# The second token block's seven Strassen factors: split ahead of time into scratch instead of at the block boundary

## The chip, the cores and the metric

One core of a Trainium2 chip runs the whole kernel. The metric is the device time of one execution in microseconds (us). Five engines work side by side and meet through semaphores: TensorE (PE, with its weight loads PEld) multiplies, VectorE (DVE) and GpSimd (POOL) do elementwise work, ScalarE (ACT) does copies and functions, SyncE (SP) issues the transfers between HBM and the on-chip memory (SBUF). Every engine takes its own instructions strictly in the order in which they were laid down.

## The reference, cut to what matters

A decoder layer: LayerNorm, a mixer (sliding-window attention beside gated linear attention), LayerNorm, then a SwiGLU feed-forward and a last LayerNorm. The change lies in the feed-forward's first half:

```python
def swiglu(h, w_gate, w_up, w_down):
    a = jax.nn.silu(jnp.einsum('bld,df->blf', h, w_gate)) * jnp.einsum('bld,df->blf', h, w_up)
    return jnp.einsum('blf,fd->bld', a, w_down)
```

Here h has 2048 tokens of 1024 features, and the gate and up matrices have 2816 columns each. All of it is float32.

## The kernel before, in words

**Two parts of a number.** A float32 value x is written as the sum of two: hi, a copy of x rounded by ACT into the type float32r, and lo = x - hi, made by DVE or POOL. A product of two such values takes three matmuls (hi hi, hi lo, lo hi). `split_into` (L182) makes both parts: its line 183 is the ACT copy, line 184 the subtraction. Nearly all splits of the kernel are counted under these two lines, so the profile's rows are told apart by the names of their tiles.

**Blocks and pairs.** The gate and up products run over two token blocks (`tb` 0 and 1) of 1024 tokens. Within a block the loop at L1411 runs over 11 *pairs* (`p`), each a group of 256 columns of the gate and of the up matrix. A pair is a Strassen-Winograd scheme: the block's activations, cut into four quarters (two halves of the features by two halves of the tokens, 512 tokens each), give seven *factors*: three quarters as they are (b11, b21, b22) and four sums or differences (t1 to t4). The weights give seven others (a11, ps2, ps1, a12, ps3, a22, ps4). `product(f)` (L1420) multiplies one factor of the activations by one of the weights: 24 matmuls of 128x128 by 128x512. The order of a pair is b11, t2, t1, b21, t3, t4, b22. DVE adds the results out of PSUM (`add`, L1435), `gate` (L1384) makes four gated activations out of them, POOL makes three further sums and one difference (L1477 to L1483), and all of it is stored for the second half of the feed-forward.

**Where the factors live.** A factor of the activations holds both its parts for four feature tiles: [128, 2, 4, 512], 2 MB. All seven lie in SBUF for a whole block. The quarters come from `n_scT`, the normalised activations, transposed, in HBM. Sums for the second block are made early by `combine_later` (L660): in the pairs p = 2 to 5 of the first block, one feature tile per pair, four quarters of [128, 512] are loaded into `cb` buffers (four of them, pool `hop4`), DVE makes the four sums in place (L671), and they are stored unsplit to `t_sc`.

**The block boundary.** In the last pair of the first block, right after `product(f)` has used a factor for the last time, `make(f, 1)` (L678) fills its place anew: for each of the four feature tiles a raw [128, 512] row is loaded into a `cb` buffer (L701 for b11, b21, b22 from `n_scT`; L704 for t1 to t4 from `t_sc`), ACT copies hi into the factor's place, and lo is made there by POOL for tiles 0 and 2 and by DVE for tiles 1 and 3 (L707). That is 28 loads, 28 copies, 14 subtractions on POOL and 14 on DVE for the seven factors.

**The weights.** `fetch_weights` (L1349) loads the four raw quarters of the next pair (512 KB each), `weights` (L1357) makes the seven factors of them: POOL does four sums (L1369, L1373) and the lo of four factors, DVE the lo of three (ps1, ps3, ps4; L1377, L1379, L1382), ACT all seven hi. Four buffers (`whl`) hold them, so they are made only a few products ahead. The profile calls the factors split from raw quarters `pa` and the others `ps`.

**What sets the order.** The framework's scheduler reorders instructions across the program by a timing model and then fixes one order per engine; instructions passed to `tc.keep_in_program_order` keep their order among themselves. All transfers of this stage go through SP's single queue, where an entry that waits (for a buffer or for its data) holds up those behind it. Results of `gate` and of the sums lie in three staging buffers (`sa`, `sb`, `sc`), so `sa` of a pair can be written only once the stores from the last pair's `sa` have landed.

Of the kernel before, what the change touches and what calls it, by code (L numbers as in the profile page):

```python
# [14 lines left out]
P = 128  # L15
# [108 lines left out]
def body(ctx, tc, t, seq):  # L124
# [11 lines left out]
    HT = TF // 2  # L136
    NTB = seq // TF
    NT = HT // P
    t_sc = [dr.tile([2, P, KT // 2, 2, HT], F32, name=f"t_sc{n}") for n in range(NTB)]

    a_sc = [[dr.tile([P, NTB, HT], F32, name=f"a_sc{i}_{p}") for p in range(NP)] for i in range(6)]
    a_last = [dr.tile([P, NP, HT], F32, name=f"a_last{n}") for n in range(NTB)]
# [494 lines left out]
    def combine(tb, k, tile_):  # L637

        def load(kh, th):
            x = tile_(f"cb{tb}_{k}_{kh}{th}")  # L640
            nc.sync.dma_start(x, quarter(tb, kh, th, k, 1)[:, 0, :])
            return x

        if tb > 0:
            yield from combine_later(tb, k, tile_)
            return
# [12 lines left out]

    def combine_later(tb, k, tile_):  # L660

        x = {}
        for kh, th in ((1, 1), (0, 1), (0, 0), (1, 0)):
            y = x[kh, th] = tile_(f"cb{tb}_{k}_{kh}{th}")
            tc.keep_in_program_order(nc.sync.dma_start(y, quarter(tb, kh, th, k, 1)[:, 0, :]))
        yield
        b22, b12, b11, b21 = x.values()
        for f, o, a, b, how in (("t3", b22, b22, b12, ALU.subtract), ("t1", b12, b12, b11, ALU.subtract),
                                ("t2", b11, b11, b22, ALU.add), ("t4", b21, b21, b11, ALU.subtract)):
            i, j = COMBINED[f]  # L670
            tc.keep_in_program_order(nc.vector.tensor_tensor(o, a, b, op=how))  # L671
            nc.sync.dma_start(t_sc[tb][i, :, k, j], o)
        yield
# [4 lines left out]
    def make(f, tb):  # L678

        if f in FIRST:  # L680
            x = hb.tile([P, 2, KT // 2, HT], F32R, tag="h16", name=f"h_{f}_{tb}", bufs=2)
        else:
            pool = pools["hop1" if f in EARLY else "hop3" if f == "b22" else "hop2"]
            x = pool.tile([P, 2, KT // 2, HT], F32R, tag=f"h_{f}", name=f"h_{f}_{tb}", bufs=1)
        if f in FIRST and tb == 0:
            for k in range(0, KT // 2, 2):
                raw = staging(f"r_{f}{tb}_{k}").rearrange("p (k q) -> p k q", q=HT)
                if f in SOURCE:
                    nc.sync.dma_start(raw, quarter(tb, *SOURCE[f], k, 2))
                else:  # L690
                    i, j = COMBINED[f]
                    nc.sync.dma_start(raw, t_sc[tb][i, :, k : k + 2, j])
                split_into(x[:, 0, k : k + 2], x[:, 1, k : k + 2], raw, nc.vector)
            return x
        for k in range(KT // 2):
            if tb > 0:
                raw = pools["hop4"].tile([P, HT], F32, tag="cb", name=f"r_{f}{tb}_{k}", bufs=4)
            else:
                raw = pools["hop1"].tile([P, HT], F32, tag="mk", name=f"r_{f}{tb}_{k}", bufs=3)
            if f in SOURCE:  # L700
                row_ = nc.sync.dma_start(raw, quarter(tb, *SOURCE[f], k, 1)[:, 0, :])  # L701
            else:
                i, j = COMBINED[f]
                row_ = nc.sync.dma_start(raw, t_sc[tb][i, :, k, j])  # L704
            if tb > 0:
                tc.keep_in_program_order(row_)
            split_into(x[:, 0, k], x[:, 1, k], raw, nc.vector if k % 2 else nc.gpsimd)  # L707
        return x

# [379 lines left out]
    for s in range(NSB):  # L1089
# [4 lines left out]
        for what in (MIXING_STEPS if nxt else LAST_STEPS).split():  # L1094
# [7 lines left out]
                start_ffn(int(what[1]))  # L1102
            elif what[0] == "C":
                if s == NSB - 2:
                    for _ in combine(0, int(what[1]), lambda n: op_.tile([P, HT], F32, tag="nt", name=n, bufs=3)):
                        pass
            else:
                take(what, nxt)
        pj = nxt
# [235 lines left out]
    hops2 = ctx.enter_context(ExitStack())  # L1345
    c2 = ctx.enter_context(ExitStack())
    quarters = {}

    def fetch_weights(p, tb):  # L1349

# [60 lines left out]
    for tb in range(NTB):  # L1411
        for p in range(NP):
# [24 lines left out]
                    nc.vector.tensor_tensor(o[i], x[i], y[i], op=ALU.add)  # L1437

            p1, u2, u4 = tl("p1", "p1"), tl("u2", "u2"), tl("u4", "u4")
            combined_ = None  # L1440
            if tb == 0 and NTB > 1 and 2 <= p < 2 + KT // 2:
                combined_ = combine(1, p - 2, lambda n: pools["hop4"].tile([P, HT], F32, tag="cb", name=n, bufs=4))
                next(combined_)
            for o, x in zip(p1, product("b11")):
                nc.scalar.activation(o, x, AF.Copy)
            add(u2, p1, product("t2"))
            add(u4, u2, product("t1"))
            add(p1, p1, product("b21"))
            if p + 1 < NP:
                fetch_weights(p + 1, tb)  # L1450
            elif tb + 1 < NTB:
# [74 lines left out]
```

## Time and profile before

| what | value |
|---|---|
| median of three runs | 2270.1 us (2267.31 to 2276.69) |
| the profiled execution's own time | 2267.38 us |
| its span in the trace | 2265.6 us |
| granted TensorE clock, mean | 0.986 |
| PE / DVE / ACT / POOL busy, whole span | 96% / 66% / 37% / 56% |

Times below are us from the start of the span unless it says otherwise. The feed-forward's first block runs up to about 1405, its second block from there to 1833.5, and the down projection follows. In a row of stretches the busy time of an engine is followed by its number of instructions; in rows of groups stand the instruction count, the busy time and the mean of one in ns, then the idle time before them and what ended it.

### The profile page before, as it was taken

The numbers are of one execution on the slowest core, as the hardware profiler recorded it, in microseconds if no ns is written. First come the engines' busy times: TensorE is split into PE (matmuls) and PEld (weight loads), VectorE is DVE, ScalarE is ACT, GpSimd is POOL, SyncE is SP. The second block draws the span as 40 slices with busy tenths as digits, with TensorE's granted clock in tenths as the row PEclk, the third lists the DMA queues.
The fourth block names the chain that finished last, engine by engine and source line by source line (L and its number), as shares of the span: only waits on it lengthen the run. The fifth ranks groups of instructions, "written<-read, shape, count | busy, mean of one in ns | idle before, by whom it ended". The sixth has DMA issues, their size and how long they took to land.

```text
span 2265.6 us, 31576 instructions
## 1 busy us (share of the span) xinstructions
PE 2170.6 (96%) x11536; PEld 1863.0 (82%) x11536; DVE 1501.0 (66%) x2437; ACT 833.8 (37%) x1450; POOL 1260.5 (56%) x974
## 2 busy tenths in 40 slices
PE   6899999999999999899999999999999999999998
PEld 5787888888899989777888888788888888888886
DVE  6665554566755678457899667876656555775687
ACT  4444554444243342343232323332222232222343
POOL 5765554564615243238877667877675634553433
PEclk9999999999999999999999999999999999999999
DMA  9868584564778586862535234333232278656463
GB/s 322 312 228 283 187 285 142 179 253 156 282 245 303 186 305 245 297 222 72 186 130 172 93 116 163 124 132 110 100 107 100 96 264 297 228 216 229 162 235 124
DMA packets 179628, 446.75 MB, mean 197 GB/s; under 512 B 16609, under 2 KB 62594, under 8 KB 167186
## 3 DMA queue, kind: packets, MB, share of 16 engines
q1 hardware_dynamic: 175666, 442.30, 56.0%
q10 hardware_dynamic: 3808, 2.45, 0.3%
q8 instruction: 91, 1.49, 0.3%
q14 instruction: 63, 0.52, 0.1%
HBM read 299.85 MB, written 144.83 MB: 196 GB/s over the span
## 4 chain that ended last, share of the span: by engine, by line
PE 45%; DVE 4%; POOL 2%; issue 2%; DMA 1%; ACT 0%; SPq 0%; POOLq 0%; DVEq 0%; ACTq 0%
PE t L195 17%; PE d L1234 16%; PE b L195 13%; DVE A L184 1%; DVE y L1140 1%; DMA r_b<-n_scT 1%; DMA r_t<-t_sc 1%; POOL pa L184 0%; DVE h_t L184 0%; DVE y L1315 0%; DVE B L184 0%; POOL a L1369 0%; POOL s L1373 0%; DVE y L1286 0%; DVE y L1309 0%
## 5 line engine op out<-in xcount | busy, mean ns | idle before, releaser
L1234 PE MATMUL d<-B,A 128*128 128x512 f32 x1848 | 419.7, 389 | 1.3 <-DVE y L1140 1.1
L1234 PEld LDWEIGHTS d<-B,A 128*128 128x128 f32 x1848 | 346.7, 188 | 74.1 <-DVE y L1140 1.6
L195 PE MATMUL t<-h_t,ps 128*128 128x512 f32 x1584 | 369.6, 391 | 2.3 <-ACT ps L183 1.8
L195 PEld LDWEIGHTS t<-h_t,ps 128*128 128x128 f32 x1584 | 298.0, 189 | 65.7 <-ACT ps L183 2.8
L195 PE MATMUL pu<-h,hl_u 128*128 128x512 f32 (+1 forms) x1008 | 245.7, 389 | 4.7 <-ACT h L183 3.5
L195 PE MATMUL b<-h_b,pa 128*128 128x512 f32 x1032 | 244.9, 393 | 4.3 <-POOL pa L184 4.3
L195 PEld LDWEIGHTS b<-h_b,pa 128*128 128x128 f32 x1032 | 195.3, 190 | 46.0 <-POOL pa L184 5.2
L184 POOL TENSOR_TENSOR pa<-a,pa 128x1024 fp32r<-128x1024 f32 x65 | 169.5, 2610 | 113.5 <-ACT pa L183 113.5
L195 PEld LDWEIGHTS pu<-h,hl_u 128*128 128x128 f32 x1008 | 178.5, 191 | 35.9 <-ACT h L183 4.1
L195 PE MATMUL po<-hl_o,msh 128*128 128x256 f32 x1024 | 199.9, 289 | 5.6 <-DVE yo L801 4.0
L184 DVE TENSOR_TENSOR A<-rA,A 128x1024 fp32r<-128x1024 f32 (+1 forms) x78 | 117.5, 1531 | 103.9 <-ACT A L183 103.9
L195 PEld LDWEIGHTS po<-hl_o,msh 128*128 128x128 f32 x1024 | 162.6, 191 | 7.3 <-DVE yo L801 6.0
L183 ACT ACTIVATE A<-rA 128x1024 fp32r<-128x1024 f32 (+1 forms) x78 | 78.7, 1042 | 212.5 <-PE d L1234 188.3
L195 PE MATMUL po<-hl_o,msl 128*128 128x256 f32 x512 | 147.3, 288 | 0.0
L1437 DVE TENSOR_TENSOR u<-u,t 128x512 f32<-128x512 f32 x132 | 89.3, 679 | 66.2 <-PE t L195 66.0
L195 PE MATMUL b<-h_b,ps 128*128 128x512 f32 x528 | 125.4, 393 | 4.9 <-ACT h_b L183 4.8
L195 PE MATMUL t<-h_t,pa 128*128 128x512 f32 x528 | 124.1, 390 | 1.2 <-POOL pa L184 1.2
L1369 POOL TENSOR_TENSOR a<-a,a 128x1024 f32<-128x1024 f32 x44 | 124.3, 2825 | 1.6
L195 PEld LDWEIGHTS b<-h_b,ps 128*128 128x128 f32 x528 | 99.8, 190 | 26.6 <-ACT h_b L183 5.0
L195 PEld LDWEIGHTS t<-h_t,pa 128*128 128x128 f32 x528 | 98.9, 188 | 22.5 <-POOL pa L184 2.0
L184 DVE TENSOR_TENSOR ps<-a,ps 128x1024 fp32r<-128x1024 f32 x44 | 82.0, 1863 | 46.2 <-ACT ps L183 46.2
L183 ACT ACTIVATE ps<-a 128x1024 fp32r<-128x1024 f32 x66 | 69.8, 1058 | 105.4 <-PE t L195 70.4
(321 smaller groups left out, 4365.6 us busy)
## 6 DMA issues: line engine op xcount, KB each, us to landing
a<-w_gu SPq DMA_DIRECT2D x88, 512.0 KB, 4.4
hl_u<-w_u SPq DMA_DIRECT2D x42, 1024.0 KB, 6.2
rA<-a_sc SPq DMA_DIRECT2D x66, 512.0 KB, 4.9
w<-w_d SPq DMA_DIRECT2D x50, 512.0 KB, 4.8
hl_o<-w_o SPq DMA_DIRECT2D x24, 1024.0 KB, 7.8
hT_sc<-h SPq DMA_DIRECT2D x32, 512.0 KB, 6.6
gh<-hT_sc SPq DMA_DIRECT2D x16, 1024.0 KB, 10.4
w_u<-hl_u SPq DMA_DIRECT2D x14, 1024.0 KB, 8.3
```

The costliest lines, as they stand in the source:

```text
L183: nc.scalar.activation(hi, src, AF.Copy)
L184: (lo_eng or nc.vector).tensor_tensor(lo, src, r32(hi), op=ALU.subtract)
L195: nc.tensor.matmul(out, l, r, start=(i == 0), stop=(i == n - 1))
L1140: return (eng or nc.vector).tensor_tensor(o, x, y, op=ALU.add)
L1234: nc.tensor.matmul(pt, a_[:, a, ca], fb[:, b, cb], start=(p == 0 and j == 0), stop=(p == NP - 1 and j == 2))
L1369: sub = lambda o, x, y: nc.gpsimd.tensor_tensor(o, x, y, op=ALU.subtract)
L1437: nc.vector.tensor_tensor(o[i], x[i], y[i], op=ALU.add)
```

## The change

The two parts of all seven factors of the second block are made during the first block and kept in HBM scratch; the boundary only loads them.

- A generator `factors_later` takes one feature tile (row k, four in all) per two pairs, over the pairs p = 1 to 8; the function `later` advances it three times in a pair: before b11, after b21 and after b22.
- In the odd pair it loads three quarters (b11, b21, b22), splits them (hi by ACT into one of the three `mk` buffers of pool `hop1`, lo by DVE in place in the `cb` buffer) and stores hi and lo to a scratch tensor `f_sc` per factor; then it loads four quarters for the sums. In the even pair it makes the four sums (DVE), then splits t1 and t4 and stores them; after b21 it splits t3 and t2 and stores them.
- `make(f, 1)` issues two loads of 1 MB straight into the factor's place, with no copy and no subtraction.
- `combine_later` and the second block's `t_sc` go. `combine` for the first block is a plain function now and does what it did.

```diff
-    t_sc = [dr.tile([2, P, KT // 2, 2, HT], F32, name=f"t_sc{n}") for n in range(NTB)]
+    t_sc = [dr.tile([2, P, KT // 2, 2, HT], F32, name="t_sc0")]
+    f_sc = {f: dr.tile([P, 2, KT // 2, HT], F32, name=f"f_sc_{f}") for f in ("b11", "b21", "b22", "t1", "t2", "t3", "t4")}
...
-    def combine_later(tb, k, tile_):
...
+    def factors_later(tb):
+        held = tc.keep_in_program_order
+
+        def load(k, which):
+            x = {}
+            for kh, th in which:
+                y = x[kh, th] = pools["hop4"].tile([P, HT], F32, tag="cb", name=f"cb{tb}_{k}_{kh}{th}_{len(which)}", bufs=4)
+                held(nc.sync.dma_start(y, quarter(tb, kh, th, k, 1)[:, 0, :]))
+            return x
+
+        def part(f, k, x):
+            y = pools["hop1"].tile([P, HT], F32R, tag="mk", name=f"hi_{f}{tb}_{k}", bufs=3)
+            lo = x.bitcast(F32R)
+            held(nc.scalar.activation(y, x, AF.Copy))
+            held(nc.vector.tensor_tensor(lo, x, r32(y), op=ALU.subtract))
+            for a, z in enumerate((r32(y), x)):
+                nc.sync.dma_start(f_sc[f][:, a, k, :], z)
+
+        def sums(x, which):
+            b22, b12, b11, b21 = x.values()
+            for f, o, a, b, how in (("t3", b22, b22, b12, ALU.subtract), ("t1", b12, b12, b11, ALU.subtract),
+                                    ("t2", b11, b11, b22, ALU.add), ("t4", b21, b21, b11, ALU.subtract)):
+                if f in which:
+                    held(nc.vector.tensor_tensor(o, a, b, op=how))
+                    yield f, o
+
+        for k in range(KT // 2):
+            x = load(k, ((0, 0), (1, 0), (1, 1)))
+            yield
+            for f, at_ in SOURCE.items():
+                part(f, k, x[at_])
+            yield
+            x = load(k, ((1, 1), (0, 1), (0, 0), (1, 0)))
+            yield
+            made = dict(sums(x, ("t3", "t1", "t2", "t4")))
+            for f in ("t1", "t4"):
+                part(f, k, made[f])
+            yield
+            for f in ("t3", "t2"):
+                part(f, k, made[f])
+            yield
+            yield
...
+        if tb > 0:
+            for k in range(0, KT // 2, 2):
+                tc.keep_in_program_order(nc.sync.dma_start(r32(x)[:, :, k : k + 2, :], f_sc[f][:, :, k : k + 2, :]))
+            return x
         for k in range(KT // 2):
-            if tb > 0:
-                raw = pools["hop4"].tile([P, HT], F32, tag="cb", name=f"r_{f}{tb}_{k}", bufs=4)
-            else:
-                raw = pools["hop1"].tile([P, HT], F32, tag="mk", name=f"r_{f}{tb}_{k}", bufs=3)
+            raw = pools["hop1"].tile([P, HT], F32, tag="mk", name=f"r_{f}{tb}_{k}", bufs=3)
...
             p1, u2, u4 = tl("p1", "p1"), tl("u2", "u2"), tl("u4", "u4")
-            combined_ = None
-            if tb == 0 and NTB > 1 and 2 <= p < 2 + KT // 2:
-                combined_ = combine(1, p - 2, lambda n: pools["hop4"].tile([P, HT], F32, tag="cb", name=n, bufs=4))
-                next(combined_)
+            def later():
+                if tb == 0 and NTB > 1 and p > 0:
+                    next(later_, None)
+
+            later()
             for o, x in zip(p1, product("b11")):
                 nc.scalar.activation(o, x, AF.Copy)
             add(u2, p1, product("t2"))
             add(u4, u2, product("t1"))
             add(p1, p1, product("b21"))
+            later()
...
             add(u4, u4, product("b22"))
-            if combined_ is not None:
-                next(combined_)
+            later()
```

More of the change, by code (lines that the diff above doesn't have):

```diff
@@ L642, in load @@
             return x
-        if tb > 0:
-            yield from combine_later(tb, k, tile_)
-            return
         def op(f, o, x, y, how):
@@ L658, in combine @@
         op("t4", b21, b21, b11, ALU.subtract)
-    def combine_later(tb, k, tile_):
[L662 to L673, printed above, removed]
+    def factors_later(tb):
[36 more added lines that the diff above has]
+            yield
@@ L1104, in body @@
                 if s == NSB - 2:
-                    for _ in combine(0, int(what[1]), lambda n: op_.tile([P, HT], F32, tag="nt", name=n, bufs=3)):
-                        pass
+                    combine(0, int(what[1]), lambda n: op_.tile([P, HT], F32, tag="nt", name=n, bufs=3))
             else:
@@ L1347, in body @@
     quarters = {}
+    later_ = factors_later(1)
     def fetch_weights(p, tb):
```

7 lines of the change are left out of this document (2 added, 5 removed).

## The prediction, made before the change was run

> **What bounds the kernel now.** I read the page's head first, then busy time by stretches, then the PE's own order of time at the block boundary, then who was waited for.
>
> ```profile
> span 2265.6 us, 31576 instructions
> PE 2170.6 (96%) x11536; PEld 1863.0 (82%) x11536; DVE 1501.0 (66%) x2437; ACT 833.8 (37%) x1450; POOL 1260.5 (56%) x974
> ```
>
> The PE is the bound, so an edit elsewhere pays only where the PE stands still. The stretches below are one pair long or nearly so: the fourth pair with early sums, one without, the last pair of the first block, and two longer stretches that hold the first two pairs of the second.
>
> ```profile
> 1176.80:1214.80 38.00, 38.00 (x169) 31.50 (x168) 34.49 (x30) 10.94 (x13) 27.39 (x13) 1.00 0.47 160
> 1291.00:1329.00 38.00, 38.00 (x169) 31.48 (x168) 23.94 (x26) 10.94 (x13) 25.82 (x13) 1.00 0.30 105
> 1367.00:1405.04 38.04, 38.04 (x170) 31.50 (x169) 24.49 (x24) 15.42 (x22) 32.37 (x18) 1.00 0.53 174
> 1405.04:1449.00 43.96, 40.17 (x164) 32.37 (x163) 37.51 (x29) 18.37 (x27) 37.91 (x20) 0.92 0.53 173
> 1449.00:1491.00 42.00, 40.28 (x177) 32.68 (x176) 33.51 (x33) 12.72 (x17) 32.59 (x14) 1.00 0.31 111
> ```
>
> Columns: length, then busy time of PE, PEld, DVE, ACT, POOL, the granted clock, the DMA share, GB/s. In the first block's pairs the PE is busy all the time, with the sums (DVE 34.49 of 38) or without (23.94). It idles only in the last two rows. There the PE's order of time gives the loss product by product; a healthy product lasts 1372.39 - 1366.95 = 5.44 us.
>
> ```profile
> 1366.95 5.60 PE L195 MATMUL b<-h_b,pa 128*128 128x512 f32 x24
> 1372.39 11.04 PE L195 MATMUL t<-h_t,ps 128*128 128x512 f32 x48
> ...
> 1421.36 0.61 PE L195 MATMUL b<-h_b,pa 128*128 128x512 f32 x2
> 1425.14 7.99 PE L195 MATMUL b<-h_b,pa 128*128 128x512 f32 x22 [3.17 <-POOL pa L184]
> 1432.97 5.60 PE L195 MATMUL t<-h_t,ps 128*128 128x512 f32 x24
> 1438.41 0.61 PE L195 MATMUL t<-h_t,pa 128*128 128x512 f32 x2
> 1439.64 5.28 PE L195 MATMUL t<-h_t,pa 128*128 128x512 f32 x22 [0.62 <-POOL pa L184]
> 1444.76 5.60 PE L195 MATMUL b<-h_b,ps 128*128 128x512 f32 x24
> ...
> 1466.52 0.61 PE L195 MATMUL b<-h_b,pa 128*128 128x512 f32 x2
> 1468.31 5.28 PE L195 MATMUL b<-h_b,pa 128*128 128x512 f32 x22 [1.18 <-POOL pa L184]
> 1473.43 5.60 PE L195 MATMUL t<-h_t,ps 128*128 128x512 f32 x24
> 1478.87 0.61 PE L195 MATMUL t<-h_t,pa 128*128 128x512 f32 x2
> 1480.03 5.32 PE L195 MATMUL t<-h_t,pa 128*128 128x512 f32 x22 [0.54 <-POOL pa L184]
> 1485.19 5.60 PE L195 MATMUL b<-h_b,ps 128*128 128x512 f32 x24
> ```
>
> Four products are late, all for a weight's lo (`pa`) from POOL. The first takes 1432.97 - 1421.36 = 11.61 us, 6.17 too many: 3.17 waiting, most of the rest because the 22 matmuls after the wait take 7.99 us where 24 usually end in 5.60 (the granted clock of that stretch is 0.92). The second takes 6.35 (0.91 too many), the third 6.91 (1.47), the fourth 6.32 (0.88). Together 9.4 us. That is the whole prize: 0.41% of the median.
>
> What made POOL late is seen in its groups, and DVE's, from 1376 to 1445:
>
> ```profile
> L184 POOL TENSOR_TENSOR h_t<-r_t,h_t 128x512 fp32r<-128x512 f32 x8 | 13.9, 1754 | 2.5 <-ACT h_t L183 2.5
> L184 POOL TENSOR_TENSOR h_b<-r_b,h_b 128x512 fp32r<-128x512 f32 x6 | 9.9, 1649 | 7.9 <-ACT h_b L183 7.9
> L184 DVE TENSOR_TENSOR h_t<-r_t,h_t 128x512 fp32r<-128x512 f32 x8 | 14.0, 1760 | 3.2 <-ACT h_t L183 3.2
> L184 DVE TENSOR_TENSOR h_b<-r_b,h_b 128x512 fp32r<-128x512 f32 x6 | 8.9, 1477 | 3.2 <-ACT h_b L183 3.2
> ```
>
> The 14 lo of the second block's factors on POOL cost 13.9 + 9.9 = 23.8 us there, and the POOL idles only 12 us in a plain pair (38.00 - 25.82). The same on DVE costs 22.9 us.
>
> **The change part by part.** *Removed at the boundary:* those 28 subtractions and 28 copies. Without 23.8 us of foreign work POOL is back at its plain 25.82 of 38 and its `pa` in time. Term 1: -9.4 us, bounds -9.4 (nothing else is lost there) and -7.1 (the third and fourth delays stay, below).
>
> *Added at the boundary:* 14 loads of 1 MB, each released by the end of a product. Seven factors of 2.1 MB are 14.7 MB; with one pair's weights (4 x 512 KB) and seven stores (256 KB) it is 18.6 MB, asked for within one pair.
>
> ```profile
> 704.00:708.00 4.00, 4.00 (x36) 4.00 (x35) 1.67 (x7) 1.36 (x2) 0.00 (x0) 1.00 1.03 418
> 1384.00:1388.00 4.00, 4.00 (x19) 3.34 (x18) 0.49 (x2) 1.94 (x3) 1.58 (x2) 1.00 0.95 305
> gh<-hT_sc SPq DMA_DIRECT2D x16, 1024.0 KB, 10.4
> 1380.77 0.33 SPq L1416 DMA_DIRECT2D a_sc<-sa  x1
> 1391.53 0.63 ACT L1385 ACTIVATE sa<-p 128x512 f32<-128x512 f32 x1 [2.33 <-DVE p L1437]
> ```
>
> The DMA engines, when full, moved 418 GB/s in one stretch and 305 in another. 18.6 MB take 44.5 or 61 us. The first place comes free at 1372.4, so the burst ends at 1417 or 1433; its last factor, b22, is first multiplied at 1405.04 + 6 x 5.44 = 1437.7. The factors come in time with 20 or 4 us left; singly, the same kind of 1 MB load (`gh`) landed in 10.4 us, against some 32 us between a place's release and its next use. What is queued behind the burst: the stores of `sa`, issued at 1380.77 and needed landed by ACT's next write of `sa` at 1391.53. One pair later that is 1418.9 and 1429.6, so with the slower rate ACT, and the weights' hi behind it, is some 4 us late. Term 2: between 0 (fast rate) and +6.2 (as much as the worst of today's delays); I take +1, nearer to 0 because a late ACT first eats the weights' lead.
>
> By the Trainium skill (DMA: Bandwidth & Descriptors, Anatomy of one DMA) a transfer costs about 2.0 us and its bytes at 436 GB/s. An estimate by that page puts the burst at 45 us and term 2 at 0; the row of 305 GB/s, with loads and stores mixed, speaks against relying on it.
>
> *Moved into the first block:* 28 subtractions, all on DVE, 28 copies on ACT, 56 stores, and 28 loads in place of 16. ACT has 27 us free per pair (10.94 busy) and gets 3.5 copies of 128x512, some 2.2 us if each takes the 0.63 of the ACT instruction of that size in the row above: nothing. Transfers: the sums pair moves 160 GB/s x 38 us = 6.1 MB; the new pair, 13 transfers in place of 8, 7.4 MB, a share near 0.57 instead of 0.47: nothing. If that cover failed, the `cb` loads would be late first, and DVE's sums behind them. On SP's queue a load for the sums waits until the `cb` buffers' stores have landed; weights and gate stores stand behind it, which have some 10 us (1380.77 to 1391.53).
>
> DVE is the part to weigh.
>
> ```profile
> L671 DVE TENSOR_TENSOR cb<-cb,cb x16: 676/1974/2782, 1105.0 to 1224.5; 128x512 f32<-128x512 f32 x16
> 1151.06 2.31 DVE L184 TENSOR_TENSOR ps<-a,ps 128x1024 fp32r<-128x1024 f32 x1
> 1160.23 5.60 PE L195 MATMUL t<-h_t,ps 128*128 128x512 f32 x24
> ```
>
> A sum takes 0.68 us undisturbed, 1.97 in the median. Four sums raise DVE from 23.94 to 34.49, 2.6 us each with what they do to their neighbours, and the PE loses nothing in four such pairs in a row. Now an odd pair gets 3 operations of this size, an even one 4 sums and 4 splits. Against eight pairs at the tested four that is 28 + 16 - 32 = 12 too many. A price c of each lies between 0.68 and 2.6; the nearest row is that of the splits at the boundary, 22.9/14 = 1.64, so about 20 us in all. What can take it: the 3.5 us in which DVE idles in a sums pair (38.00 - 34.49, hand-overs with ACT), over eight pairs 28 us, say half usable as the new operations are ready long before; and 6.9 us of lead (the lo of ps3 ends at 1153.37 and is used at 1160.23). 14 + 6.9 = 20.9 covers 20, barely, and an even pair's 4 x 1.64 = 6.6 just fits the lead. Term 3: between 0 (c at 0.68) and 12 x 2.6 - 6.9 = +24 (nothing usable); no gain is possible, as the PE was full there. I take +2.
>
> Sum: 2267.4 - 9.4 + 1 + 2 = 2261.0 for an execution like the profiled one. The median of the runs shown lies 2.7 above that; I add it and forecast 2264.
>
> **The rivals.** *VectorE falls behind in the first block (slower).* Place: pairs 2, 4, 6 and 8 of the first block, where eight operations meet DVE's 24 us. If DVE can't use its hand-overs, c = 1.64 costs 20 - 6.9 = 13 us, 2272 in all with terms 1 and 2 (2274.7 as a median); c = 2.6 costs 24, 2283, as a median 2286. It decides from c = 20.9/12 = 1.74 us. For it speaks how a DVE operation with both inputs in SBUF waits while POOL works: the same gate step takes 2.7 or 0.7 us.
>
> ```profile
> 1161.89 2.67 DVE L1387 SCALAR_TENSOR_TENSOR sa<-sa,p 128x512 f32<-128x512 f32 x1
> 1161.62 2.39 POOL L184 TENSOR_TENSOR pa<-a,pa 128x1024 fp32r<-128x1024 f32 x1 [3.48 <-ACT pa L183]
> 1275.40 0.69 DVE L1387 SCALAR_TENSOR_TENSOR sa<-sa,p 128x512 f32<-128x512 f32 x1
> ```
>
> If these exclude each other wholly, the even pair asks for POOL's 25.82, 8 gate steps and 8 sums and splits of 0.69 and three lo of weights (128x1024, twice the length, some 1.4): 25.8 + 11.0 + 4.1 = 40.9 of 38.1, 2.8 us too many, four times 11 us if the odd pairs (37.5) can't take it: 2267.4 - 9.4 + 1 + 11 = 2270.0, as a median 2272.7. Against it: the even pairs' lateness can be carried over, which leaves 11 - 4 x 0.6 - 6.9 = 2.
>
> The Trainium skill (SBUF — State Buffer, Who interferes with whom) states just this: the pair of ports that VectorE shares with GpSimd is an exclusive lock, and the loser is fully blocked. By that rule the sum would be 2272.7 where lateness isn't carried, by the price of the boundary's rows 2264; the 2.67 beside the 0.69 agrees with it.
>
> *The burst of loads replaces the stall.* At 305 GB/s with weights and stores in between, a factor or the `sa` hand-over is late by about what POOL is now; 6.2 us come back: 2267.4 - 9.4 + 6.2 + 2 + 2.7 = 2269. For it: 18.6 MB in 38 us would be 489 GB/s, more than any row. Against: the loads have a further pair to land.
>
> *It doesn't do all it says.* The second pair's delays may come from SP's queue rather than from POOL's extra work:
>
> ```profile
> 1411.86 15.81 SPq L704 DMA_DIRECT2D r_t<-t_sc  x8
> 1429.58 0.33 SPq L1355 DMA_DIRECT2D a<-w_gu  x1
> ```
>
> Eight loads held the queue until 1427.7, and the next weights were issued at 1429.58. If the new loads, waiting in the same queue for the PE, hold weights up the same way, only 7.1 us go: 2267.4 - 7.1 + 1 + 2 + 2.7 = 2266.
>
> **How the numbers follow.** Forecast 0.53; VectorE behind 0.22; burst 0.13; half done 0.12. Half a per cent, 11.35 us, is about what a measurement of this kernel can tell from no change. Faster than 2258.7 needs the whole prize and luck in the runs, as even 2258.0 + 2.7 = 2260.7 falls short: 0.08. Slower than 2281.5 needs c near 2.6: 0.12. Within: 0.80. The forecast's own range is 2258 to 2268; the range that also takes in the rivals to the middle of the first is 2257.5 to 2279.
>
> **What would show it.** Right: no PE wait for `pa` between 1405 and 1491, no `h_t`/`h_b` splits there, the second block's pairs 38.1 us long, and 38.0 of 38 PE in the pairs 1 to 8 with DVE near 36. Term 2 wrong: PE or ACT waiting for `f_sc` or `a_sc` transfers at the boundary. Term 3 wrong: PE waiting for `ps` of DVE, or for PSUM, in even pairs of the first block.

## The result, and the profile after

The changed kernel takes 2294.9 us (median of six, 2284.2 to 2302.8), the kernel before on the same chip 2273.5 (median of six, 2267.3 to 2276.7): a ratio of 1.0097 with a 95% interval of 1.0071 to 1.0122. It is 1% slower, and the whole interval lies above 1. The forecast was 2264, its range 2257.5 to 2279, and "slower" had a chance of 0.12.

The profiled execution took 2292.8 us against 2267.4, 25.4 more. Here are the page's head, then four stretches with the columns of before (length; busy time of PE, PEld, DVE, ACT, POOL; granted clock, DMA share, GB/s): pairs 7 and 8 of the first block, then its last pair and the first pair of the second block.

```profile
span 2291.0 us, 31641 instructions
PE 2183.2 (95%) x11536; PEld 1870.5 (82%) x11536; DVE 1516.1 (66%) x2451; ACT 829.9 (36%) x1450; POOL 1231.8 (54%) x960
```

```profile
1278.30:1316.40 38.10, 38.10 (x170) 31.55 (x169) 24.27 (x23) 10.35 (x14) 23.75 (x11) 1.00 0.44 149
1316.40:1363.90 47.50, 41.40 (x170) 32.94 (x169) 43.72 (x40) 14.02 (x19) 29.95 (x13) 0.93 0.48 163
...
1402.00:1440.00 38.00, 38.00 (x169) 31.49 (x168) 27.16 (x27) 11.23 (x14) 27.20 (x13) 1.00 0.69 246
1440.00:1478.10 38.10, 38.10 (x169) 31.55 (x169) 24.89 (x26) 11.28 (x14) 26.95 (x13) 1.00 0.90 355
```

The boundary is healed: the PE is full in both its pairs, where it lost 9.4 us before. The loss has moved into the first block. Pair lengths, from one b11 product to the next in the PE's order of time, are 38.1 us in a healthy pair; pairs 2, 4, 6 and 8 now take 44.5, 47.3, 47.9 and 47.5, the odd pairs 38.1. That is 6.4 + 9.2 + 9.8 + 9.4, before rounding 34.9 us lost, less 9.4 won: the 25.4 us of the two profiles, to a tenth. In what follows "the loss" is this sum over the even pairs. It is the measure used for the experiments too, because pair 1 began anywhere from 1016 to 1033 us in the profiled executions, though the change touches nothing ahead of it; a single total carries that spread and a pair length does not.

Where pair 8 loses its 9.4 us stands in the PE's order of time, its fifth product being that of t3 with the weights' factor ps3:

```profile
1316.37 5.60 PE L196 MATMUL b<-h_b,pa 128*128 128x512 f32 x24
1321.81 11.04 PE L196 MATMUL t<-h_t,ps 128*128 128x512 f32 x48
1332.69 0.61 PE L196 MATMUL b<-h_b,pa 128*128 128x512 f32 x2
1334.70 5.30 PE L196 MATMUL b<-h_b,pa 128*128 128x512 f32 x22 [1.40 <-POOL pa L185]
1344.05 1.22 PE L196 MATMUL t<-h_t,ps 128*128 128x512 f32 x2 [4.05 <-ACT ps L184]
1345.92 7.25 PE L196 MATMUL t<-h_t,ps 128*128 128x512 f32 x22 [0.66 <-DVE ps L185]
1353.01 5.60 PE L196 MATMUL t<-h_t,pa 128*128 128x512 f32 x24
```

A healthy pair would start this product at 1316.37 + 4 x 5.44 = 1338.13. It starts 5.92 late, waiting for ps3's hi from ACT, and takes 1353.01 - 1344.05 = 8.96 us instead of 5.44: 5.9 + 3.5 = 9.4. The 3.5 are a second wait, for the lo from DVE, and 22 slow matmuls after it (the granted clock is 0.93 over this pair, and 0.66 over the 8.95 us from 1344.05).

Why ps3 is late is told by the chain of waits, followed back from that product. Columns: start, length, what. From where these lines begin, in pair 7, the chain does not touch the PE until 1345.92:

```profile
1298.96 0.32 SPq L1443
1299.33 4.75 DMA cb<-n_scT
...
1312.22 3.48 DVE cb L674 x2
...
1325.48 0.32 SPq L1443
...
1326.82 4.20 DMA cb<-n_scT
...
1332.35 2.85 DVE cb L683
...
1341.95 0.61 ACT hi_t L673
...
1343.05 0.95 ACT ps L184
1344.04 0.70 DVE cb L674
1344.73 1.15 DVE ps L185
1345.92 12.69 PE t L196 x46
```

The links shown from 1299.33 to 1344.04 are the change's own work, standing in a queue ahead of old work, or the weight's hi and the store between them; the pieces left out are for the most part the adds and gate steps of the pair, late by then. In the odd pair SP issues the three quarters only at 1299.33, 21 us into the pair, behind the last store of the pair before (L1443); the hi copies for them already stand at the head of ACT's order, and behind them a weight's hi. The same stretch in ACT's and DVE's orders of time:

```profile
1304.16 0.63 ACT L673 ACTIVATE hi_b<-cb 128x512 fp32r<-128x512 f32 x1 [13.68 <-DMA cb<-n_scT]
1304.70 1.04 ACT L184 ACTIVATE ps<-a 128x1024 fp32r<-128x1024 f32 x1
```

```profile
1305.78 1.23 DVE L185 TENSOR_TENSOR ps<-a,ps 128x1024 fp32r<-128x1024 f32 x1 [10.28 <-ACT ps L184]
...
1309.57 6.14 DVE L674 TENSOR_TENSOR cb<-cb,hi_b 128x512 fp32r<-128x512 f32 x3
...
1327.88 1.74 DVE L1413 SCALAR_TENSOR_TENSOR sa<-sa,u 128x512 f32<-128x512 f32 x1 [0.70 <-ACT sa L1412]
...
1332.35 9.03 DVE L683 TENSOR_TENSOR cb<-cb,cb 128x512 f32<-128x512 f32 x4
1341.30 3.43 DVE L674 TENSOR_TENSOR cb<-cb,hi_t 128x512 fp32r<-128x512 f32 x2
1344.66 1.21 DVE L185 TENSOR_TENSOR ps<-a,ps 128x1024 fp32r<-128x1024 f32 x1
```

ACT stands 13.68 us, DVE behind it 10.28; then DVE makes up arrears with three lo on top (6.14 us). Pair 8's first gate step (`sa<-sa,u`) runs at 1327.88, 11.5 us after the pair's start. Then come four sums (9.03) and two lo (3.43), and only then the lo of ps3, 28.3 us into the pair; the PE wants it 21.8 us in.

The volume would fit: over pairs 7 and 8 DVE is busy 24.27 + 43.72 = 68.0 us, and two healthy pairs last 76.2.

### The profile page after: what moved, and what is told of

It is laid out like the page before. It is cut to its first block, busy times and chain, and to the rows that moved or that the text cites. A ratio compares the mean times of both kernels' runs of the same rounds, so it can differ in the third digit from the quotient of the medians.

```text
span 2291.0 us, 31641 instructions
## 1 busy us (share of the span) xinstructions
PE 2183.2 (95%) x11536; PEld 1870.5 (82%) x11536; DVE 1516.1 (66%) x2451; ACT 829.9 (36%) x1450; POOL 1231.8 (54%) x960
## 4 chain that ended last, share of the span: by engine, by line
PE 38%; DVE 7%; issue 3%; POOL 3%; DMA 2%; ACT 1%; SPq 0%; POOLq 0%; DVEq 0%; ACTq 0%
PE d L1260 16%; PE t L196 13%; PE b L196 9%; DVE cb L683 2%; DMA cb<-n_scT 1%; DVE y L1166 1%; DVE cb L674 1%; POOL pa L185 1%; DVE A L185 1%; POOL a L1396 0%; DMA a_sc<-sc 0%; DVE ps L185 0%; DVE sb L1414 0%; DVE u L1464 0%; POOL sc L1505 0%
## 5 line engine op out<-in xcount | busy, mean ns | idle before, releaser
L196 PE MATMUL t<-h_t,ps 128*128 128x512 f32 x1584 | 381.2, 399 | 19.4 <-ACT ps L184 15.4
L196 PEld LDWEIGHTS t<-h_t,ps 128*128 128x128 f32 x1584 | 304.3, 193 | 88.8 <-ACT ps L184 18.1
L185 DVE TENSOR_TENSOR A<-rA,A 128x1024 fp32r<-128x1024 f32 (+1 forms) x78 | 122.8, 1599 | 100.9 <-ACT A L184 100.9
L185 DVE TENSOR_TENSOR ps<-a,ps 128x1024 fp32r<-128x1024 f32 x44 | 74.1, 1684 | 67.5 <-ACT ps L184 67.5
L196 PE MATMUL pv<-hl_vg,gh 128*128 128x256 f32 (+1 forms) x768 | 105.3, 292 | 0.8 <-ACT lt L890 0.6
```

What stands on the lines that cost most here:

```text
L185: (lo_eng or nc.vector).tensor_tensor(lo, src, r32(hi), op=ALU.subtract)
L196: nc.tensor.matmul(out, l, r, start=(i == 0), stop=(i == n - 1))
```

## The experiments

All are edits of the changed kernel. Where a part of the computation is left out, the text says which.

**1. The splits later.** In the even pair only the sums are laid down before b11; t1 and t4 are split after b21, t3 and t2 after b22.

```diff
             made = dict(sums(x, ("t3", "t1", "t2", "t4")))
+            yield
             for f in ("t1", "t4"):
...
             yield
-            yield
```

> The same work as the changed kernel, but in the even pairs the four sums stand alone before b11; t1 and t4 are split after b21 and t3 and t2 after b22. Theory A (ScalarE in order: the hi copies of t1 and t4 stand on ScalarE ahead of the hi of the weights' ps3 and wait for VectorE's sums): the copies find their sums ready, the waits of TensorE for ps3's hi (four of about 4 us in the changed kernel) go, and of the 34.9 us lost in the first block at most 10 stay: about 2258 to 2268 beside 2267 of the kernel before. Rival B (VectorE is simply too full in the even pairs, its lo are late whatever ScalarE does): 25 us or more stay, 2283 to 2293.

Measured: 2288.9 us, ratio 1.0064 (1.0039 to 1.0089) to the kernel before; loss 4.1 + 10.0 + 8.6 + 9.5 = 32.2 us of 34.9. The edit moved only half of what it names. On VectorE the first of the moved lo in pair 8 now runs at 1348.09, behind that of ps3 at 1340.76; but in the order fixed for ScalarE two copies still stand ahead of ps3's hi, waiting for the sums:

```profile
1334.13 0.64 ACT L673 ACTIVATE hi_t<-cb 128x512 fp32r<-128x512 f32 x1 [7.63 <-DVE cb L683]
1338.61 0.63 ACT L673 ACTIVATE hi_t<-cb 128x512 fp32r<-128x512 f32 x1 [3.84 <-DVE cb L683]
...
1339.62 1.05 ACT L184 ACTIVATE ps<-a 128x1024 fp32r<-128x1024 f32 x1
```

So this run does not test the copies of the even pairs, as it was meant to. It shows that the two lo ahead of ps3 are not the whole cause: without them there the loss is almost the same, while ACT still waits for the sums, and 45.3 us for `cb` loads in the odd pairs.

**2 and 3. One half of each split alone.** One kernel leaves the 28 lo out (what is stored as lo is the unsplit value), one the 28 hi copies (DVE subtracts a row from itself, and that is stored for both parts).

```diff
-            held(nc.vector.tensor_tensor(lo, x, r32(y), op=ALU.subtract))
```

```diff
-            held(nc.scalar.activation(y, x, AF.Copy))
-            held(nc.vector.tensor_tensor(lo, x, r32(y), op=ALU.subtract))
+            held(nc.vector.tensor_tensor(lo, x, x, op=ALU.subtract))
```

> Left out: the 28 subtractions that make lo in the first block (the unsplit row is stored in its place). Sums and ScalarE copies stand as in the changed kernel. Theory A: the copies still wait for the sums, so TensorE still waits for the hi of ps3 in pairs 2, 4, 6, 8 and 20 us or more of the 34.9 stay: 2278 to 2292. Rival B: VectorE is back at the load of the kernel before, nothing is lost: 2258 to 2262.

> Left out: the 28 ScalarE copies that make hi in the first block (a subtraction of the row from itself keeps VectorE's load, and its result is stored twice). Theory A: ScalarE no longer waits for sums, at most 10 of the 34.9 us stay: 2258 to 2268. Rival B: VectorE has the same work, 25 us or more stay: 2283 to 2293.

Measured: without lo the loss is 1.5 + 3.2 + 5.3 + 1.9 = 11.9 us (2268.9 us in all), without hi 7.2 + 5.4 + 5.4 + 5.3 = 23.3 (2286.6). 11.9 + 23.3 = 35.2, close to the 34.9 of both, though no run shows that the two parts add up. The kernel with the copies alone, which the prediction costed at nothing, loses a third: they are 28 of some 0.62 us, 17 us of ACT's time, but they stop ACT for far longer. The waits of the kernel without lo (total, times, longest):

```profile
ACT hi_b L672 <- DMA cb<-n_scT: 39.5, 3, 14.0
ACT hi_t L672 <- DVE cb L681: 38.5, 7, 7.7
```

**4. The copies on VectorE.** No ScalarE instruction can then stand waiting for a load or a sum.

```diff
-            held(nc.scalar.activation(y, x, AF.Copy))
+            held(nc.vector.tensor_copy(y, x))
```

> The 28 hi copies are made by VectorE in place of ScalarE, at the same places. Theory A: ScalarE no longer waits for sums; VectorE has 4 copies more per even pair, some 0.4 to 0.7 us each without a second SBUF input: 5 to 15 us lost, 2263 to 2273. Rival B: VectorE is fuller still, more than 35 us lost: above 2293.

Measured: 2289.0 us, loss 8.5 + 8.4 + 8.4 + 6.5 = 31.8. The PE now waits for DVE's `ps`, 23.1 us in all, instead of ACT's: for each split DVE has two operations ahead of ps3, a copy and a subtraction, where it had one. Moving the work to the other engine only moved the wait.

**5. The splits behind ps3 and into the next pair.** t1 and t4 are split after b22, t3 and t2 at the start of the next pair.

```diff
         for k in range(KT // 2):
+            for f in ("t3", "t2") if made else ():
+                part(f, k - 1, made[f])
             x = load(k, ((0, 0), (1, 0), (1, 1)))
...
             made = dict(sums(x, ("t3", "t1", "t2", "t4")))
-            for f in ("t1", "t4"):
-                part(f, k, made[f])
             yield
-            for f in ("t3", "t2"):
-                part(f, k, made[f])
             yield
+            for f in ("t1", "t4"):
+                part(f, k, made[f])
```

> The same work, but in the even pairs only the sums stand before b11; t1 and t4 are split after b22, t3 and t2 at the start of the next pair, so that neither a copy nor a subtraction of them is written ahead of the weights' ps3 and ps4 of the pair. Theory C (VectorE has no slack from the odd pair's three lo to ps3 in the even pair, so it is what stands ahead of ps3 that costs): 5 to 15 us lost in the first block, 2263 to 2273. Rival D (the sum of the work over two pairs is too much wherever it stands): 25 us or more, 2283 and above.

Measured: 2280.8 us, loss 1.3 + 5.4 + 2.4 + 5.4 = 14.5. Place alone, with not one operation less, takes 20 us off.

**6 and 7. GpSimd's part.** One kernel makes the 28 lo on GpSimd. One leaves out GpSimd's four sums of the weights in every pair, so that raw quarters are split in place of the sums.

```diff
-            held(nc.vector.tensor_tensor(lo, x, r32(y), op=ALU.subtract))
+            held(nc.gpsimd.tensor_tensor(lo, x, r32(y), op=ALU.subtract))
```

```diff
-        s1 = fp.tile([P, D], F32, tag="s1", name=f"s1_{nm}", bufs=1)
+        s1 = a21
...
-        nc.gpsimd.tensor_tensor(s1, a21, a22, op=ALU.add)
-        sub(a21, a11, a21)
-        sub(a11, s1, a11)
...
-        sub(a12, a12, a11)
```

> The 28 lo are made by GpSimd in place of VectorE, at the same places. Theory C: VectorE is back at the sums alone and the part of its lo goes; what ScalarE's copies cost by waiting in order (11.9 us where the lo were left out) stays, GpSimd has room for 3.5 lo of 1.3 to 1.7 us per pair: 2268 to 2275. Rival D: GpSimd and VectorE exclude each other, it doesn't matter which of them makes the lo: 2283 and above.

> Left out: GpSimd's four sums of the raw weights in every pair (the raw quarters are split in their place), 2.4 to 2.8 us each, so GpSimd works some 10 us less per pair. If VectorE's new operations take 2.2 to 2.7 us because they wait while GpSimd works, they take 1.6 or less here and at most 15 of the 34.9 us stay: below 2273. If their length is not GpSimd's doing, they keep it and 25 us or more stay: 2283 and above.

Measured: with lo on GpSimd 2281.2 us, loss 9.4 + 5.7 + 7.8 + 2.6 = 25.5, the PE waiting 14.2 us for GpSimd's `pa`. Without the weights' sums 2264.5 us, and every pair is 38.1 us long: loss 0, with all 28 splits in their places. The operations of the changed kernel, then of the one without the sums, from the view of the tile (ns of one: least, median, most):

```profile
L683 DVE TENSOR_TENSOR cb<-cb,cb x16: 1641/2222/2880, 1074.4 to 1339.7; 128x512 f32<-128x512 f32 x16
L674 DVE TENSOR_TENSOR cb<-cb,hi_t x16: 1749/2250/2884, 1083.4 to 1354.6; 128x512 fp32r<-128x512 f32 x16
L674 DVE TENSOR_TENSOR cb<-cb,hi_b x12: 678/2730/2880, 1060.1 to 1315.0; 128x512 fp32r<-128x512 f32 x12
```

```profile
L683 DVE TENSOR_TENSOR cb<-cb,cb x16: 679/1666/1671, 1075.7 to 1305.6; 128x512 f32<-128x512 f32 x16
L674 DVE TENSOR_TENSOR cb<-cb,hi_t x16: 678/1233/2884, 1081.4 to 1320.0; 128x512 fp32r<-128x512 f32 x16
L674 DVE TENSOR_TENSOR cb<-cb,hi_b x12: 678/685/2886, 1055.6 to 1282.5; 128x512 fp32r<-128x512 f32 x12
```

Without GpSimd's sums the medians of the subtractions fall from 2.25 and 2.73 us to 1.23 and 0.69, that of VectorE's sums from 2.22 to 1.67. How the price comes about stands in the changed kernel's trace, here a lo of VectorE beside an instruction of GpSimd:

```profile
1061.93 2.88 DVE L674 TENSOR_TENSOR cb<-cb,hi_b 128x512 fp32r<-128x512 f32 x1
1061.71 2.55 POOL L185 TENSOR_TENSOR ps<-a,ps 128x1024 fp32r<-128x1024 f32 x1 [4.45 <-DMA f_sc_b<-hi_b]
```

GpSimd's ends at 1064.26, VectorE's 0.55 us behind it. Of the 44 operations in the three rows of the changed kernel, 39 take more than 1.6 us: each of them begins while an instruction of GpSimd runs and ends 0.55 us after the end of one. The other five take 0.68 us and meet none. So the price in DVE's time is GpSimd's doing. This is what the Trainium skill (SBUF — State Buffer, Who interferes with whom) states of the pair of ports that VectorE shares with GpSimd, an exclusive lock; these rows agree. Experiment 7 does not separate that price from another effect of leaving the sums out: the weights' factors, too, are ready earlier.

**8. The loads earlier.** The three quarters of the next row are loaded at the end of the even pair, half a pair ahead of their place in the change.

```diff
+        x = load(0, ((0, 0), (1, 0), (1, 1)))
+        yield
         for k in range(KT // 2):
-            x = load(k, ((0, 0), (1, 0), (1, 1)))
-            yield
...
             yield
+            if k + 1 < KT // 2:
+                x = load(k + 1, ((0, 0), (1, 0), (1, 1)))
+            yield
```

> The same work; only the three quarters of a row for b11, b21, b22 are loaded half a pair earlier, at the end of the pair before. In the changed kernel ScalarE stands some 10 us per odd pair at the hi copy of b11 until its load lands. Theory E (that wait is the root: all behind it is late, VectorE idles 10 us and enters the even pair late): at most 10 of the 34.9 us stay, 2258 to 2268. Theory C: some 23 us stay, as with the ScalarE copies left out: 2278 to 2284.

Measured: 2282.0 us, loss 6.2 + 0.4 + 4.8 + 1.5 = 12.9. ACT waits 3.3 us for these loads instead of 40.3. In pair 2, whose row is loaded at the same place as in the change, nothing changes (6.2 against 6.4); in the other three the loss falls from 28.5 to 6.7. What is left stands in DVE's order in pair 6, which began at 1233.1:

```profile
1240.30 1.73 DVE L1416 SCALAR_TENSOR_TENSOR sa<-sa,u 128x512 f32<-128x512 f32 x1 [0.70 <-ACT sa L1415]
...
1244.76 9.09 DVE L683 TENSOR_TENSOR cb<-cb,cb 128x512 f32<-128x512 f32 x4
1253.77 3.46 DVE L674 TENSOR_TENSOR cb<-cb,hi_t 128x512 fp32r<-128x512 f32 x2
1257.15 1.21 DVE L185 TENSOR_TENSOR ps<-a,ps 128x1024 fp32r<-128x1024 f32 x1
```

The first gate step comes 7.2 us into the pair, no longer 11.5; the 9.1 + 3.5 us of sums and lo are unchanged, and ps3's lo starts 24.0 us in.

**9 and 10. Both together, and fewer, longer instructions.** Experiment 9 puts the early load and the later splits together. Of two others, 10 splits several rows in one instruction (three quarters; t1 with t4; t3 with t2) with the early load, and 10c does so in the later places.

```diff
-            for f, at_ in SOURCE.items():
-                part(f, k, x[at_])
+            part(("b11", "b21", "b22"), k, x[:, 0:3])
...
-            for f in ("t1", "t4"):
-                part(f, k, made[f])
+            part(("t1", "t4"), k, x[:, 1::2])
```

> Two edits together: three quarters of each row are loaded half a pair earlier, and in the even pair only the sums stand ahead of the second matmul block, the splits of t1 and t4 behind the third and those of t3 and t2 behind the last. Theory (two causes that add up: a ScalarE copy that waits in its queue for a late load, and VectorE's chain ahead of the third product of the even pair): the load alone left 12.9 us of 34.9, and the later splits take most of that, so even pairs lose 0 to 6 us in all. Rival (the even pair has no room for these operations wherever they stand, VectorE being slowed throughout by GpSimd's sums): the loss stays at 12 us or more, with PE waiting for VectorE's ps at the pair's end instead.

> Early load, and the splits of several rows made in one instruction: three source rows in one copy and one subtraction, t1 and t4 in one of each, t3 and t2 in one of each (7 pairs of operations a row become 3); the sums stay four. Theory (an instruction of VectorE with two inputs waits for one instruction of GpSimd to end, so the price goes by the number of instructions): lo operations fall from 7 to 3 a row, 28 to 12 in all, some 10 us of VectorE less in the four rows, and even pairs lose 0 to 5 us against 12.9 with the early load alone. Rival (the price goes by the bytes): one merged subtraction takes two or three times a single one, about 4 to 7 us, and the loss stays at 10 us or more.

> Early load, merged operations, and the later places of the even pair together. Theory: even pairs lose 0 to 2 us, the time is the kernel before less the boundary's 9.4 us, some 2262 us. Rival (bytes, not instructions, set VectorE's price): 5 us or more stay in the even pairs, and nothing is won against the early load with later places alone.

Measured: loss in the even pairs 4.1 + 5.3 + 3.3 + 6.7 = 19.4 us for experiment 9, and 1.6 more in odd ones (2280.3 us); 17.8 and 1.6 for 10 (2275.8); 14.3 for 10c (2279.0). All three theories of the loss fell: none comes below the 12.9 of the early load alone. In 9 and 10c the load stands behind the splits, which had been moved to the end of the pair, so it is no longer early: ACT again waits 30.9 and 28.9 us for DMA. As in experiment 1, copies of the even pairs also still stand ahead of ps3's hi there. The price did go by the instruction more than by the bytes:

```profile
L677 DVE TENSOR_TENSOR cb<-cb,mk_all 128x1024 fp32r<-128x1024 f32 x8 | 22.3, 2792 | 4.6 <-ACT mk_all L676 4.6
L677 DVE TENSOR_TENSOR cb<-cb,mk_all 128x1536 fp32r<-128x1536 f32 x4 | 11.8, 2952 | 0.0
```

Three rows in one take 2.95 us, one row alone 2.2 to 2.7 in the median. All lo of the four rows together cost 34.1 us of DVE. But a merged copy starts only when all its sums are there, and ps3 waits behind it, 23.5 to 25.1 us into the pair.

**11 and 12. Half the change, four operations a pair at most.** Experiment 11 makes the sums in pairs 2 to 5 as the kernel before did, unsplit, and splits the three quarters in pairs 6 to 9; t1 to t4 are split at the boundary. Experiment 12 makes and splits t1 to t4 only, the sums in the odd pair and their splits in the even one after it, and splits the quarters at the boundary:

```diff
+        x = load(0, ALL4)
+        yield
         for k in range(KT // 2):
...
             made = dict(sums(x, ("t3", "t1", "t2", "t4")))
+            yield
+            yield
             for f in ("t1", "t4"):
                 part(f, k, made[f])
             yield
             for f in ("t3", "t2"):
                 part(f, k, made[f])
             yield
+            if k + 1 < KT // 2:
+                x = load(k + 1, ALL4)
+            yield
             yield
```

> Half of the change, laid out so that no pair gets more than four operations: the four sums of a row in pairs 2 to 5, stored unsplit as in the kernel before; the three quarters b11, b21, b22 split in pairs 6 to 9, one row a pair, loaded a half pair ahead. The boundary loads those three in both parts and splits t1 to t4 there, 16 copies and 16 subtractions instead of 28. Theory (a pair carries three or four such operations for nothing, seven or eight not, since VectorE pays over 2 us for each beside GpSimd): all pairs of the first block 38.1 us, no loss; at the boundary GpSimd has 8 foreign subtractions instead of 14 and the loss falls from 9.4 to 0 to 4 us. Time 5 to 9 us under the kernel before of the same batch, less what runs vary. Rival (any split beside the weights' work costs, by its place in ScalarE's and VectorE's order): pairs 6 to 9 lose 3 us or more each, 12 in all.

> The other half, spread: the four sums of a row in an odd pair, their four splits in the even pair that follows (t1 and t4 before the first product, t3 and t2 after the fourth), the next row loaded at that pair's end; the quarters are split at the boundary, 12 copies and 12 subtractions instead of 28. Theory (four operations a pair are free and the copies find their sums made long before): pairs 1 to 8 lose 0 to 2 us in all, the boundary 0 to 4 instead of 9.4. Rival (splits ahead of ps3's cost whatever stands beside them): the even pairs lose 3 us or more each, as the early load alone did in its worse pairs (4.8 and 6.2).

Measured: 2268.0 and 2266.4 us, beside 2269.7 for the kernel before. In 11 the first block loses 1.1 us, in pair 7, but its boundary loses 9.9, as much as ever; that part of the theory fell. The PE's four waits there are all for GpSimd (1.64 us for `ps`, 0.42 and 2.79 for `pa`, 1.68 for the lo of a factor, `h_t`). In 12 the first block loses nothing and the boundary 1.8:

```profile
1438.52 0.61 PE L196 MATMUL t<-h_t,pa 128*128 128x512 f32 x2
1440.61 5.28 PE L196 MATMUL t<-h_t,pa 128*128 128x512 f32 x22 [1.48 <-POOL pa L185]
```

An even pair of experiment 12, from 1220.9 on, in DVE's order:

```profile
1228.13 1.74 DVE L1419 SCALAR_TENSOR_TENSOR sa<-sa,u 128x512 f32<-128x512 f32 x1 [0.70 <-ACT sa L1418]
...
1232.62 4.58 DVE L674 TENSOR_TENSOR cb<-cb,hi_t 128x512 fp32r<-128x512 f32 x2
1238.17 2.38 DVE L185 TENSOR_TENSOR ps<-a,ps 128x1024 fp32r<-128x1024 f32 x1 [0.98 <-issue]
```

The first gate step is at 7.2 us, as in experiment 8, but only two lo stand before that of ps3, which starts 17.3 us in. The lo are no cheaper than in the change (16 of them 38.7 us, 2.4 each) and the pair loses nothing. The sums, now alone in the odd pairs, are cheaper, 0.68 us in the median instead of 2.22, with GpSimd's work on the weights as it was:

```profile
L683 DVE TENSOR_TENSOR cb<-cb,cb x16: 678/684/2293, 1066.3 to 1293.1; 128x512 f32<-128x512 f32 x16
```

ACT's order in the same even pair:

```profile
1235.53 0.63 ACT L673 ACTIVATE hi_t<-cb 128x512 fp32r<-128x512 f32 x1 [4.92 <-DVE cb L674]
...
1237.03 1.06 ACT L184 ACTIVATE ps<-a 128x1024 fp32r<-128x1024 f32 x1
```

A copy still waits ahead of ps3's hi, 4.92 us: no longer for a load or a sum but for a lo of VectorE (three buffers hold the hi, and this is the fourth). It does no harm here, as ps3's hi is still in time.

**13. Timed, and with b11 ahead as well.** Experiment 12 in rounds, and beside it the same with b11 split ahead too, its four rows in pair 9.

```diff
-            yield
-            yield
+                yield
+                yield
+        x = [load(k, ((0, 0),))[0, 0] for k in range(KT // 2)]
+        yield
+        for k in range(KT // 2):
+            part("b11", k, x[k])
+            if k % 2:
+                yield
```

> The kernel of the run before, timed in rounds. By its trace no pair of the first block loses anything and the boundary loses 1.8 us instead of 9.4: 7.6 us under the kernel before, ratio 0.9966. If the single time of that run was luck of the stages before the feed-forward, the ratio is 0.999 or above.

> As that kernel, with b11 split ahead too, its four rows in pair 9: 8 copies and 8 subtractions are left at the boundary. Theory (up to four operations in a pair are free): pair 9 loses nothing and the boundary's last 1.8 us go, 9.4 us under the kernel before, ratio 0.9959. Rival (the boundary's rest comes from the loads in SP's queue): the boundary keeps 1 to 2 us and the ratio stays at 0.9966.

Measured: experiment 12 takes 2263.4 us, ratio 0.9944 (0.9920 to 0.9968); with b11 2262.6 us, ratio 0.9935 (0.9911 to 0.9958). Both are faster than the kernel before, and so than the change. Pair 9 loses nothing, and the boundary of the second loses 1.4 us; in this execution of experiment 12 it lost 3.9, in the one above 1.8. The traces thus account for 5.5 to 8.0 us of gain; the medians lie 12.0 and 12.7 apart, and what the rest is, beyond the spread of the stages ahead, stays open. The two kernels can't be told apart by these runs.

## Why the prediction was wrong, step by step

*What bounds the kernel, and term 1* were right to a tenth in size: the 9.4 us at the boundary went with the splits; the bound of -7.1 is out. That they were owed to GpSimd's foreign work alone is not shown, as DVE's subtractions, the copies and the 28 small loads went at the same time.

*Term 2* was +1 with bounds 0 and 6.2; it is 0. The burst came at 246 and 355 GB/s in the two pairs shown above, and the PE waited for none of it. The fit cited there from the Trainium skill (DMA: Bandwidth & Descriptors, Anatomy of one DMA) is given on that page for transfers that GpSimd issues; SP issued these, and the measured rates decide.

*Term 3* failed: 34.9 us instead of +2, beyond its own upper bound of 24. Three of its steps failed.

First, "28 + 16 - 32 = 12 too many": the step counted operations per pair, as if a place for four of them, once shown to be free, were free wherever they stand. In the runs below the loss goes by when ps3's lo starts. For the even pairs, from DVE's and the PE's orders of time:

| kernel | first gate step, us into the pair | ps3's lo starts, us into the pair | loss of the pair, us |
|---|---|---|---|
| before, pairs 4 to 6 | 0.1 to 0.2 | 12.5 to 12.6 | 0 |
| after, pairs 4, 6, 8 | 10.5 to 11.6 | 27.3 to 28.4 | 9.2 to 9.8 |
| 1, later splits, pairs 4, 6, 8 | 12.1 to 13.6 | 27.8 to 29.2 | 8.6 to 10.0 |
| 2, no lo, pairs 4, 6, 8 | 6.4 to 8.4 | 22.7 to 24.6 | 1.9 to 5.3 |
| 3, no hi, pairs 4, 6, 8 | 5.5 to 5.6 | 22.4 to 22.5 | 5.4 |
| 5, splits behind, all four | 7.5 to 10.1 | 21.0 to 23.6 | 1.3 to 5.4 |
| 7, no weights' sums, all four | 0.8 to 3.3 | 13.0 to 15.7 | 0 |
| 8, early load, pairs 4, 6, 8 | 4.4 to 7.2 | 21.3 to 24.0 | 0.4 to 4.8 |
| 12, sums' factors only, all four | 7.0 to 7.9 | 17.0 to 17.7 | 0 |

Up to 17.7 us nothing is lost; from 21 us on every one of these pairs loses, and mostly the more the later ps3's lo is. The even pairs of experiments 4, 9, 10 and 10c fit in: ps3's lo starts at 22.6 to 27.8, and they lose 1.8 to 8.5. Those of experiment 6 do not (17.5 to 22.9, lost 2.6 to 9.4), because there the PE waits chiefly for GpSimd's `pa`. Experiments 8 and 12 begin their even pairs much alike and differ in what stands ahead of ps3, besides the quarters' twelve splits that 12 leaves at the boundary. So "an even pair's 4 x 1.64 = 6.6 just fits the lead" was the wrong sum: what stands ahead of ps3 there is four sums and two lo, 9.0 + 3.4 = 12.5 us. The lead of 6.9 itself had been read in a pair of before in which DVE's first gate step stood at 0.2 us; in the change's pairs 4, 6 and 8 it stands at 10.5 to 11.6.

Second, "ACT has 27 us free per pair ...: nothing", and the same for the loads. The engine's free time was real, the order was not looked at. A copy that waits for a load or a sum stops every weight's hi behind it. The prediction itself asked that for SP's queue ("weights and gate stores stand behind it") and answered with 10 us of slack; the three quarters were issued 21 us into the pair, behind the stores of the pair before. Loading earlier alone took 21.8 of the 28.5 us off pairs 4, 6 and 8. The kernel with the 28 copies and no lo lost 11.9.

Third, the price: c was taken as 1.64; lo cost 2.25 and 2.73 in the median, sums 2.22 instead of 1.97. By the prediction's own formula a price of 2.6 explains 24 us, not 34.9. The mis-sized price alone isn't the cause: experiments 5 and 8 keep every operation and the price (medians of 2.0 to 2.7 for lo, 2.2 for sums), and lose 14.5 and 12.9. For the same reason the count of twelve too many isn't the cause alone. Experiment 12 cannot decide this, since it has no more than four operations in any pair, which the prediction's count gives for nothing at any price.

The rival "VectorE falls behind" named the right sign, the right pairs (2, 4, 6 and 8) and the right engines; its point of decision, c = 1.74, was passed. Its mechanism covers the part after the late entry into the pair, not what made the entry late. Of the signs announced, "PE waiting for `ps` of DVE" came as a wait for ACT's `ps`, because ps3's hi stood behind the copies that waited for DVE's sums. The rivals of the burst and of the change half done are refuted by the full pairs at the boundary.

Open: how the 34.9 us part between the order and GpSimd's share in the price, since experiment 7 takes the price and hastens the weights at once, and experiments 5 and 8 each won over 20 us by themselves; whether all 28 splits beside the 16 sums fit for nothing in any order, since no run that keeps them and GpSimd's sums did so; and why experiment 11, with 8 instead of 14 foreign subtractions on GpSimd, still lost 9.9 us at the boundary, all of its waits being for GpSimd. Its refill loads stand behind the last pair's stores in SP's queue, which was not tried apart.

## What to carry to other kernels

Cost moved work by its place in each engine's order, not by that engine's free time: list for every moved instruction what it waits for and which due result stands behind it. A lead read from a trace holds only for the order it was read in. Here the sixteen splits of t1 to t4 were free once their sums were made a pair ahead, so that no copy waited for a load or a sum, and only two of their lo stood ahead of that of the due factor; the quarters' splits were left where they had been.

## What the runs showed of the hardware that was not expected

After a wait, matmuls may run slower: the 22 after waits of 4.05 and 0.66 us took 7.25 us, those after one wait of 1.40 us took 5.30. It added some 2 us to pair 8's delay. And in these traces a sum or a subtraction of VectorE that begins while GpSimd works waits for GpSimd's instruction to end, and then takes its own time: it ended 0.55 us after it for 128x512 in the change, and in experiment 10 1.08 us after it for 128x1024 and 1.62 for 128x1536. Merging rows saves waits, so 128x1536 took 2.95 us in the mean where one 128x512 took 2.25 or 2.73 in the median.
